# Rebuilding the first layer's attention: both branches of a head at once, stacked float32r scores, mask on TensorE, division by fours of heads, adaLN rows shared between engines

## The chip, the core and the metric

The kernel runs on one core of a Trainium2 chip. A core has five engines, each with an instruction queue of its own that is worked off in order: TensorE (PE, matrix products; PEld is its weight load), VectorE (DVE), ScalarE (ACT), GpSimd (POOL) and SyncE (SP, which here issues the DMA transfers). The metric is the device time of one execution in microseconds (us).

## What is computed

A stack of four layers on 256 tokens of 1024 features, all float32. The change is in the first: adaLN, a "native sparse" attention with three branches, and an output projection.

```python
h = rms_norm(x, g) * (1 + scale) + shift      # shift, scale, gate = silu(c) @ w_ada + b_ada
u = h @ w_in                                  # q, k/v of three branches, z, gate logits
q: 16 heads of 64;  k, v: 2 groups of 8 heads
o_cmp = softmax(q k_cmp^T, 15 compressed keys) v_cmp
o_slc = softmax(rope(q) rope(k_s)^T, causal) v_s     # all blocks are selected at this length
o_win = softmax(rope(q) rope(k_w)^T, causal) v_w     # the window is longer than the text
o = gates[0] * o_cmp + gates[1] * o_slc + gates[2] * o_win
x = x + gate * ((o * silu(z)) @ w_out)
```

With 256 tokens the second and third branch have the same form and the same causal mask and differ in keys and values alone. While the heads run, the kernel also makes the rows of adaLN that come next: 1024 columns each of the first layer's gate and the second layer's scale and shift, silu(c) @ w + b.

## The kernel before

**Weights.** Products with weights are made of float32r parts: `make` loads a unit of 1024 floats per partition (512 KB, tile `wr`), ACT copies it to the high part (`wh`, L210), DVE subtracts for the low part (`wl`, L211), and three products add up (L239, L240, L243). Five units are loaded ahead and eight split ahead. All loads are issued by SP in order; a load whose buffer is still read holds those behind it.

**Order.** The code is emitted in program order, and a scheduler puts each instruction into its engine's queue by priority; `first(ATTN)` moves the heads' instructions 1200 places ahead of what was emitted before, so that dense products (of z) fill in between. Within a queue nothing overtakes.

**The stage before the heads.** q is copied from PSUM, rotated (`rope`: three products on DVE and a sum, L408, on POOL where it is 512 wide), and both q (`qp`) and rotated q (`qr`) are transposed, four 128-blocks at a time. Keys are rotated and transposed into `kT`. Compressed keys (`kbd`) and values (`vbd`) come from small products. `cmp_probs(tok, g)` gives the probabilities of a group's eight heads over compressed keys, transposed (`cT`); it runs for group 1 before the heads and for group 0 in the middle of group 1.

**A head** (`nsa_head`). For each of two branches: `scores` does one fp32 product for the first block of 128 queries (128 keys) and one for the second (256 keys), with 64 contraction rows (L417). `shifted` (L427) adds the mask, negates and takes the least value in one DVE instruction per block, with a read of the accumulator. `exps` (L433) runs on ACT with a sum as a by-product. The sums are inverted, multiplied by the gates, and each probability block is scaled, 128 columns on DVE (L830), 256 on ACT (L828). `av` transposes three blocks (L440), copies them from PSUM on ACT (L443) and does three products with the values (L446 to L448) into `o`, where all branches and eight heads of a group add up, the compressed branch first (`cmp_part`, L808).

**AdaLN rows** (`ada_rows`, `ada`). A half row (512 columns) is a sum over eight chunks of 128 features. A transfer holds two chunks (512 KB, tile `ar`, L542), and `ARAW = 3` of them are loaded ahead through three buffers. A call of `ada` does one item: two scaled additions on DVE (L562, L564) into `ac`, and the load that takes the freed buffer. After four items one product with ones (L569) sums over partitions, and DVE adds the bias. There are 24 items; two follow each head of group 1, one each head of group 0.

**After the heads.** o is multiplied by silu(z) in `zs` (L856), transposed (L289), split, and `project_out` multiplies it by `w_out` (first product L239). Then the second layer begins, with dense products.

Of the kernel before, what the change touches and what calls it, by code (L numbers as in the profile page):

```python
# [8 lines left out]
F32 = mybir.dt.float32  # L9
# [7 lines left out]
D = 1024  # L17
# [77 lines left out]
def body(ctx: ExitStack, tc: tile.TileContext, A: dict, out: bass.AP, stop=None):  # L95
# [17 lines left out]
    # ---- PSUM banks: each kind of tile goes round its own banks  # L113
# [12 lines left out]
    # ---- constants  # L126
# [15 lines left out]
    junk = cp.tile([128, D], BF, name="junk")  # L142
# [36 lines left out]
    # ---- weights: streamed in order, split exactly into two float32r parts  # L179
    specs, made = [], []  # L180
    state = {"next": 0, "live": 0, "gate": None, "hold": False, "group": 2}
# [17 lines left out]
    def make():  # L199
# [11 lines left out]
        dve.tensor_sub(lo, raw[:, :nk * n], hi.bitcast(F32))  # L211
# [35 lines left out]
    def dense_cols(xts, nk, n, sink, kind="mm"):  # L247
        """a group of n columns of x @ W, block of tokens after block of tokens; the sink takes them from PSUM"""
# [10 lines left out]
    # ---- transposed operands  # L259
# [25 lines left out]
    def to_T(src, n, xt, k0):  # L285
        """n blocks of 128 columns, transposed and split, to chunks k0.. of xt"""
# [9 lines left out]
    def transposes(dst, srcs, eng, width=128):  # L296
        """up to four [128, width] blocks, transposed to dst [width, n, 128]"""
# [12 lines left out]
    # ---- norms  # L310
# [6 lines left out]
    def rms_rstd(src, n, eps=1e-6):  # L317
        s = small(1)
        act.activation(junk[:, :n], src, AF.Square, accum_out=s)
        return rstd_of(s, 1.0 / n, eps)  # L320
# [4 lines left out]
    def deepnorm(layer, which, last=False):  # L325
        """the sink of a product that closes a sublayer: x <- LN(alpha x + p) * g + b, and its transposed parts"""
# [28 lines left out]
    def gated(tok, h, p, g, tp):  # L355
        """x += p * g"""
# [4 lines left out]
    def halves_sumsq(tok, h, s):  # L361
        act.activation(junk[:, half(h)], x[tok][:, half(h)], AF.Square, accum_out=s[:, h:h + 1])
# [28 lines left out]
    # ---- rotations  # L391
# [3 lines left out]
    def rope(dst, src, H, hd, cos, sin, tp):  # L395
        """dst = rotated src; src [128, H, 2*hd], dst the same or with copies side by side"""
# [26 lines left out]
    def shifted(s, added, n2, tp, scale=1.0):  # L423
        """-scale * (s + added), and its least value of each block of queries"""
# [11 lines left out]
    def av(e, v, o, c0, start, eng, tp, stop=True):  # L436
        """o[tok][:, c0:c0+64] += e of the block times v(block of keys)"""
# [93 lines left out]
    def ada_rows(rows, new, ahead):  # L531
# [13 lines left out]
        def step(after=None):  # L545
# [20 lines left out]
            if u < 3:  # L566
                return
# [291 lines left out]
    for _ in range(24):  # L859
        ada()  # L860
# [438 lines left out]
```

## Time and profile before

| | |
|---|---|
| median of three runs | 1026.41 us (1024.37, 1026.41, 1039.41) |
| profiled execution, span | 1024.7 us |
| PE busy | 978.7 us, 96% |
| DVE busy | 662.3 us, 65% |
| ACT busy | 508.4 us, 50% |
| POOL busy | 39.0 us, 4% |

The profile shows one execution by its span; what a run's time has beyond it is 1.7 us against the median. Busy shares are means over stages that have different limits, so the stretches are read one by one: up to 60 us the first adaLN rows and columns, 60 to 105 rotations and compression, 105 to 210 the heads, and from there the projection and the other layers. A row of the timeline gives start, length, engine, line, operation, what it writes and reads, how many instructions are joined, and in brackets the idle time ahead of it with what ended it.

### The profile page before, as it was taken

The page shows a single profiled execution, that of the slowest core. Times are in us where ns is not written, and L with a number is a line of the kernel's source. Part 1 is how long each engine was busy: PE and PEld are TensorE (multiplying, and loading weights), DVE is VectorE, ACT ScalarE, POOL GpSimd, SP SyncE. Part 2 cuts the span into 40 slices and gives each one's busy share as a digit, 9 for nine tenths or more (in the row PEclk, how much of TensorE's full clock was granted, in tenths as well). Part 3 has the DMA queues.
Part 4 walks back from the last instruction along what each step waited for, and adds up shares of the span by engine and source line. Part 5 has one row for each costly group of instructions (what it writes and reads, how often), then busy time and mean ns, then how long its engine had stood idle before and what let it go on. Part 6 is the DMA issues. An engine that isn't in the chain of part 4 may idle for free.

```text
span 1024.7 us, 16049 instructions
## 1 busy us (share of the span) xinstructions
PE 978.7 (96%) x6068; PEld 852.1 (83%) x6068; DVE 662.3 (65%) x1304; ACT 508.4 (50%) x967; POOL 39.0 (4%) x41
## 2 busy tenths in 40 slices
PE   5988999999999999999999999999999999999997
PEld 5877687777777878978899999978997789999995
DVE  5888788848776678665855555476454495544554
ACT  5584566734545536584343443335664344433440
POOL 1002000001220001000000000000000000000000
PEclk9998898999999999999999999999999999999999
DMA  9995776434865335632356455556543335455441
GB/s 287 309 308 182 249 241 201 129 101 134 261 191 179 119 102 190 229 103 64 99 208 205 165 194 206 176 171 190 170 145 99 112 117 192 165 202 189 165 144 42
DMA packets 106173, 177.75 MB, mean 173 GB/s; under 512 B 8816, under 2 KB 40688, under 8 KB 106096
## 3 DMA queue, kind: packets, MB, share of 16 engines
q1 hardware_dynamic: 106096, 176.72, 53.5%
q8 instruction: 48, 0.79, 0.3%
q14 instruction: 29, 0.24, 0.1%
HBM read 175.65 MB, written 1.05 MB: 172 GB/s over the span
## 4 chain that ended last, share of the span: by engine, by line
PE 83%; DVE 8%; DMA 4%; ACT 3%; issue 1%; SPq 0%; DVEq 0%; POOL 0%; ACTq 0%; POOLq 0%
PE ps L239 13%; PE ps L240 13%; PE ps L243 13%; PE ps L277 9%; PE ps L278 9%; PE ps L279 9%; PE ps L417 6%; PE ps L440 2%; DMA wr<-in_ada_w_dram 2%; PE ps L446 2%; DVE wl L211 2%; PE ps L447 2%; PE ps L448 2%; PE ps L289 1%; PE ps L300 1%
## 5 line engine op out<-in xcount | busy, mean ns | idle before, releaser
L211 DVE TENSOR_TENSOR wl<-wr,wh 128x1024 fp32r<-128x1024 f32 (+5 forms) x276 | 322.9, 1204 | 155.1 <-ACT wh L210 153.9
L210 ACT ACTIVATE wh<-wr 128x1024 fp32r<-128x1024 f32 (+5 forms) x276 | 270.5, 1022 | 168.2 <-PE ps L243 74.8
L277 PE MATMUL ps<-xh,wh 128*128 128x256 f32 x736 | 209.1, 284 | 0.0
L279 PE MATMUL ps<-xh,wl 128*128 128x256 f32 x736 | 208.9, 284 | 0.0
L278 PE MATMUL ps<-xl,wh 128*128 128x256 f32 x736 | 208.5, 283 | 0.0
L240 PE MATMUL ps<-wl,xh 128*128 128x512 f32 (+5 forms) x544 | 201.3, 373 | 0.4 <-DVE wl L211 0.4
L239 PE MATMUL ps<-wh,xh 128*128 128x512 f32 (+5 forms) x544 | 197.8, 376 | 3.9 <-ACT xh L292 2.6
L243 PE MATMUL ps<-wh,xl 128*128 128x512 f32 (+5 forms) x544 | 173.4, 372 | 1.0 <-DVE xl L293 0.8
L277 PEld LDWEIGHTS ps<-xh,wh 128*128 128x128 f32 x736 | 141.1, 192 | 0.5
L278 PEld LDWEIGHTS ps<-xl,wh 128*128 128x128 f32 x736 | 141.1, 192 | 0.3
L279 PEld LDWEIGHTS ps<-xh,wl 128*128 128x128 f32 x736 | 141.1, 192 | 0.1
L239 PEld LDWEIGHTS ps<-wh,xh 128*128 128x128 f32 x544 | 104.3, 193 | 22.7 <-ACT xh L292 6.2
L240 PEld LDWEIGHTS ps<-wl,xh 128*128 128x128 f32 x544 | 105.7, 194 | 16.1 <-issue 1.2
L243 PEld LDWEIGHTS ps<-wh,xl 128*128 128x128 f32 x544 | 101.1, 192 | 18.4 <-DVE xl L293 2.9
L239 PE MATMUL ps<-wh,hh 128*128 128x512 f32 x176 | 68.6, 390 | 0.0
L240 PE MATMUL ps<-wl,hh 128*128 128x512 f32 x176 | 68.6, 390 | 0.0
L243 PE MATMUL ps<-wh,hl 128*128 128x512 f32 x176 | 68.5, 389 | 0.0
L433 ACT ACTIVATE e<-e,sm 128x128 f32<-128x128 f32 x112 | 49.7, 446 | 19.7 <-DVE sm L427 19.5
L427 DVE CUSTOM_DVE_ANT_0 e<-ps,mask 128x128 f32<-128x128 f32 (+1 forms) x144 | 45.2, 352 | 20.4 <-PE ps L417 11.4
L292 ACT ACTIVATE xh<-ps 128x512 fp32r<-128x512 f32 x36 | 20.9, 597 | 75.0 <-PE ps L289 74.7
L314 POOL TENSOR_TENSOR sm<-sm,nhalf 128x1 f32<-128x1 f32 x18 | 12.7, 706 | 856.0 <-DVE sm L313 856.0
L564 DVE SCALAR_TENSOR_TENSOR ac<-ar,cs,ac 128x512 f32<-128x512 f32 x56 | 41.7, 745 | 1.0 <-DMA ar<-in_ada_w_dram 0.7
(319 smaller groups left out, 1230.8 us busy)
## 6 DMA issues: line engine op xcount, KB each, us to landing
wr<-in_ffn_w_gate_dram SPq DMA_DIRECT2D x44, 512.0 KB, 4.7
wr<-in_ffn_w_up_dram SPq DMA_DIRECT2D x44, 512.0 KB, 4.7
wr<-in_ffn_w_down_dram SPq DMA_DIRECT2D x44, 512.0 KB, 4.7
ar<-in_ada_w_dram SPq DMA_DIRECT2D x32, 512.0 KB, 4.5
wr<-in_dil_w_in_dram SPq DMA_DIRECT2D x32, 512.0 KB, 4.5
wr<-in_cd_w_in_dram SPq DMA_DIRECT2D x22, 512.0 KB, 4.7
wr<-in_ada_w_dram SPq DMA_DIRECT2D x32, 256.0 KB, 5.1
wr<-in_nsa_w_in_dram SPq DMA_DIRECT2D x12, 512.0 KB, 5.5
```

The source lines that it names most:

```text
L210: act.activation(hi, raw[:, :nk * n], AF.Copy)
L211: dve.tensor_sub(lo, raw[:, :nk * n], hi.bitcast(F32))
L239: pe.matmul(p, lhsT=xt[0][:, k, :], rhs=w[0][:, kw, c], start=start and t == 0, stop=False)
L240: pe.matmul(p, lhsT=xt[0][:, k, :], rhs=w[1][:, kw, c], start=False, stop=False)
L243: pe.matmul(p, lhsT=xt[1][:, k, :], rhs=w[0][:, kw, c], start=False, stop=stop and t == n - 1)
L277: pe.matmul(o, lhsT=w[0], rhs=xh[:, k, :], start=k == 0, stop=False)
L278: pe.matmul(o, lhsT=w[0], rhs=xl[:, k, :], start=False, stop=False)
L279: pe.matmul(o, lhsT=w[1], rhs=xh[:, k, :], start=False, stop=k == 7)
L417: pe.matmul(p[:, c0:c1], lhsT=qT(tok), rhs=kT[:, :c1 - c0], start=True, stop=masks is None)
L427: state["dve"] = dve.tensor_tensor_reduce(out=e[:, c0:c1], in0=s[:, c0:c1], in1=added[:, 256 - (c1 - c0):], scale=-scale, scalar=3e38, op0 ...
L433: act.activation(e[:, c0:c1], e[:, c0:c1], AF.Exp, bias=n2[:, i:i + 1], scale=-1.0, accum_out=den[:, i:i + 1])
L564: dve.scalar_tensor_tensor(ac, raw[:, j, :], cs[:, k:k + 1], ac, op0=ALU.mult, op1=ALU.add)
```

## The change

**Scores.** Rotated q is split into a high and a low float32r part that lie side by side per head, so that a transpose gives 128 rows, [high; low], of one head (`qhl`). Keys of both branches stand twice along the rows, in a high (`kh`) and a low part (`kl`). A head's scores of a block of queries for both branches are one product with `kh`, one with `kl` and one bf16 product that adds the mask (`identb` times `causal01`). Two heads go together (`nsa_pair`), over three PSUM banks: `x` for the second block of each head, `y` for the first blocks of both.

**Softmax.** Three DVE reductions per pair give the maxima, and the exponentials read PSUM directly. Probabilities are not scaled: each head and branch has columns of its own in `o` for four heads, and `nsa_close` divides: a reciprocal, gates, one product per block of tokens, additions to the compressed part `oc` (on POOL for group 1, on DVE for group 0), and the product with `zs`. Of four copies of transposed probabilities three are on DVE.

**Compressed branch.** All four `cmp_probs` come before the heads.

**AdaLN rows.** 48 items of 256 KB, one chunk each, through three buffers as before; the first three chunks of a half row are scaled on ACT in place and added on POOL, the other five stay on DVE. Six items follow each pair, in program order, and no longer behind a named DVE instruction. **w_out**: the low parts of its eight units are made on POOL (`slow` is that matrix). `rms_rstd` works in two halves.

```diff
-        dve.tensor_sub(lo, raw[:, :nk * n], hi.bitcast(F32))
+        (pool if W is slow else dve).tensor_sub(lo, raw[:, :nk * n], hi.bitcast(F32))
...
-        items = [(r, h, u) for r in rows for h in range(2) for u in range(4)]
+        items = [(r, h, u) for r in rows for h in range(2) for u in range(8 // wide_k)]
...
+                    if k < shared:
+                        act.activation(raw[:, j, :], raw[:, j, :], AF.Copy, scale=cs[:, k:k + 1])
+                        if k == 1:
+                            pool.tensor_add(ac, at["r0"], raw[:, j, :])
+                        elif k:
+                            pool.tensor_add(ac, ac, raw[:, j, :])
+                        at["r0"] = raw[:, j, :]
+                    elif k == 0:
...
-        transposes(qr[tok][g], blocks(qq), dve)
+        flat = wide("hl")
+        hl = flat.rearrange("p (h a d) -> p h a d", h=8, a=2)
+        act.activation(hl[:, :, 0].bitcast(F32R), by_head(qq), AF.Copy)
+        dve.tensor_sub(hl[:, :, 1], by_head(qq), hl[:, :, 0])
+        for i in range(2):
+            transposes(qhl[tok][g][:, i * 4:i * 4 + 4, :], [flat[:, (i * 4 + j) * 128:(i * 4 + j + 1) * 128] for j in range(4)], (act, dve)[i])
...
+    with first(ATTN):
+        for g in (1, 0):
+            for tok in range(2):
+                cmp_probs(tok, g)
...
+    def nsa_scores(g, hh):
+        xs, y = [ps("x"), ps("x")], ps("y")
+        for j in range(2):
+            for tok, (p, n) in enumerate(((y[:, j * 256:(j + 1) * 256], 128), (xs[j], 256))):
+                q = qhl[tok][g][:, hh + j, :]
+                p3 = p.rearrange("p (b k) -> p b k", b=2)
+                pe.matmul(p3, lhsT=q, rhs=kh[:, g, :, :n], start=True, stop=False)
+                pe.matmul(p3, lhsT=q, rhs=kl[:, g, :, :n], start=False, stop=False)
+                pe.matmul(p3[:, :, n - 128:n], lhsT=identb, rhs=causal01.to_broadcast([128, 2, 128]), start=False, stop=True)
+        return xs, y
...
-                   lambda: pC.tile([128, D], F32, tag="araw", bufs=ARAW, name=nm("ar")), ARAW)
+                   lambda: pC.tile([128, 512], F32, tag="araw", bufs=ARAW, name=nm("ar")), ARAW, 1, 3)
...
-            for hh in range(8):
-                nsa_head(g, hh, o)
-                for _ in range(1 + g):
-                    ada(state["dve"])
+            for quad in range(2):
+                o = [ps("o"), ps("o")]
+                den = pC.tile([128, 2, 4, 2], F32, tag="den", bufs=2, name=nm("den"))
+                for pair in range(2):
+                    nsa_pair(g, quad * 4 + pair * 2, den, o)
+                    for _ in range(6):
+                        ada()
+                nsa_close(g, quad, den, o, pool if g else dve)
```

How the queues change is shown at three places. DVE's queue before, in the early heads of group 1: the scaled additions (L564, two per `ar` tile) stand between masked reductions (L427) of several heads, with weight splits (L211) among them.

```order
L211 TENSOR_TENSOR wl_1280<-wr_1277,wh_1279 128x1024
L427 ISA e_1371,sm_1370<-ps_1367,mask 128x128
L427 ISA sm_1370 128x1
L427 ISA e_1371,sm_1370<-ps_1367,mask 128x256
L427 ISA sm_1370 128x1
L564 SCALAR_TENSOR_TENSOR ac_1347<-ar_1166,cs,ac_1347 128x512 x2
L473 SCALAR_TENSOR_TENSOR zs_120<-th_1295,ps_1246 128x512
L564 SCALAR_TENSOR_TENSOR ac_1347<-ar_1350,cs,ac_1347 128x512
L211 TENSOR_TENSOR wl_1292<-wr_1289,wh_1291 128x1024
L819 RECIPROCAL sm_1357<-sm_1356 128x4
L427 ISA e_1417,sm_1416<-ps_1413,mask 128x128
L427 ISA sm_1416 128x1
```

DVE's queue in the changed kernel, after the copies of the first pair's transposed probabilities (`eT`, L451): the first half row's five scaled additions (L577, one per `ar` tile), the first steps of a division, then the next pair's copy and the reductions (L864, L862) of the pair after it.

```order
L451 COPY eT_1451<-ps_1447 128x384
L451 COPY eT_1460<-ps_1456 128x384
L577 SCALAR_TENSOR_TENSOR ac_1468<-ar_1470,cs,ac_1468 128x512
L880 RECIPROCAL rd_1578<-den_1399 128x16
L577 SCALAR_TENSOR_TENSOR ac_1468<-ar_1474,cs,ac_1468 128x512
L884 TENSOR_TENSOR rd_1578<-rd_1578,gates 128x8 x2
L577 SCALAR_TENSOR_TENSOR ac_1468<-ar_1478,cs,ac_1468 128x512
L577 SCALAR_TENSOR_TENSOR ac_1468<-ar_1481,cs,ac_1468 128x512
L577 SCALAR_TENSOR_TENSOR ac_1468<-ar_1484,cs,ac_1468 128x512
L451 COPY eT_1526<-ps_1522 128x384
L864 TENSOR_REDUCE sm_1610<-ps_1595 128x2
L862 TENSOR_REDUCE sm_1610<-ps_1597 128x4
```

The five additions of a half row now each name another `ar` tile and stand in one run ahead of a copy and of the reductions of the pair that follows.

SP's queue before, where the loads of adaLN rows begin.

```order
L205 DMA wr_1829<-in_nsa_w_out_dram 128x2x512
L542 DMA ar_1162<-in_ada_w_dram 128x2x512
L542 DMA ar_1164<-in_ada_w_dram 128x2x512
L542 DMA ar_1166<-in_ada_w_dram 128x2x512
L542 DMA ar_1350<-in_ada_w_dram 128x2x512
L205 DMA wr_1841<-in_nsa_w_out_dram 128x2x512
L542 DMA ar_1354<-in_ada_w_dram 128x2x512
L205 DMA wr_1853<-in_nsa_w_out_dram 128x2x512
L205 DMA wr_1865<-in_nsa_w_out_dram 128x2x512
L542 DMA ar_1402<-in_ada_w_dram 128x2x512
L205 DMA wr_2323<-in_dil_w_in_dram 128x2x512
```

SP's queue in the changed kernel at the same place.

```order
L207 DMA wr_1825<-in_nsa_w_out_dram 128x2x512
L548 DMA ar_1305<-in_ada_w_dram 128x512
L548 DMA ar_1307<-in_ada_w_dram 128x512
L548 DMA ar_1309<-in_ada_w_dram 128x512
L548 DMA ar_1470<-in_ada_w_dram 128x512
L548 DMA ar_1474<-in_ada_w_dram 128x512
L548 DMA ar_1478<-in_ada_w_dram 128x512
L548 DMA ar_1481<-in_ada_w_dram 128x512
L548 DMA ar_1484<-in_ada_w_dram 128x512
L548 DMA ar_1487<-in_ada_w_dram 128x512
L548 DMA ar_1555<-in_ada_w_dram 128x512
L207 DMA wr_1837<-in_nsa_w_out_dram 128x2x512
```

A load was two chunks and has become one; twice as many stand between the loads of `w_out` and of the next layer (`wr`).

POOL's queue before, from the last rotation of the first layer on: nothing stands between that and the second layer's small powers (L314) and rotations (L408).

```order
L408 TENSOR_TENSOR q_881<-rt_883,rt_884 128x512
L408 TENSOR_TENSOR q_950<-rt_952,rt_953 128x512
L314 TENSOR_TENSOR sm_2411<-sm_2411,nhalf 128x1
L314 TENSOR_TENSOR sm_2468<-sm_2468,nhalf 128x1
L408 TENSOR_TENSOR qq_2558<-rt_2559,rt_2560 128x512
```

POOL's queue in the changed kernel after the same rotation (now L414).

```order
L414 TENSOR_TENSOR q_988<-rt_990,rt_991 128x512
L570 TENSOR_TENSOR ac_1468<-ar_1305,ar_1307 128x512
L572 TENSOR_TENSOR ac_1468<-ac_1468,ar_1309 128x512
L213 TENSOR_TENSOR wl_1349<-wr_1346,wh_1348 128x1024
L213 TENSOR_TENSOR wl_1361<-wr_1358,wh_1360 128x1024
L213 TENSOR_TENSOR wl_1373<-wr_1370,wh_1372 128x1024
L570 TENSOR_TENSOR ac_1563<-ar_1487,ar_1555 128x512
L213 TENSOR_TENSOR wl_1385<-wr_1382,wh_1384 128x1024
L572 TENSOR_TENSOR ac_1563<-ac_1563,ar_1558 128x512
L891 TENSOR_TENSOR oc_1303<-oc_1303,nt_1582 128x256 x2
```

The additions of adaLN rows (L570, L572), the low parts of `w_out` (L213) and the closing additions (L891) stand one behind the other there, three low parts ahead of the second half row's first addition.

## Rows read from the trace of the kernel before

**Rows 1.** The page's chain of work that ended last: shares by engine.

```profile
PE 83%; DVE 8%; DMA 4%; ACT 3%; issue 1%; SPq 0%; DVEq 0%; POOL 0%; ACTq 0%; POOLq 0%
PE ps L239 13%; PE ps L240 13%; PE ps L243 13%; PE ps L277 9%; PE ps L278 9%; PE ps L279 9%; PE ps L417 6%; PE ps L440 2%; DMA wr<-in_ada_w_dram 2%; PE ps L446 2%; DVE wl L211 2%; PE ps L447 2%; PE ps L448 2%; PE ps L289 1%; PE ps L300 1%
```

**Rows 2.** Busy us by stretch (length, PE, PEld, DVE, ACT, POOL, granted clock, DMA).

```profile
60.00:105.00 45.00, 37.41 (x224) 30.91 (x222) 39.19 (x61) 29.09 (x49) 7.51 (x4) 0.92 0.72 226
105.00:210.00 105.00, 100.43 (x566) 76.51 (x567) 84.80 (x293) 69.51 (x219) 0.00 (x0) 0.90 0.60 195
210.00:320.00 110.00, 108.39 (x516) 85.95 (x515) 81.52 (x128) 54.60 (x90) 16.23 (x10) 1.00 0.57 177
```

**Rows 3.** The same columns for two stretches within the heads.

```profile
111.00:119.00 8.00, 8.00 (x28) 6.19 (x27) 5.49 (x23) 3.39 (x11) 0.00 (x0) 0.50 0.52 182
160.00:169.00 9.00, 9.00 (x32) 6.57 (x32) 5.56 (x23) 5.17 (x19) 0.00 (x0) 0.51 0.71 226
```

**Rows 4.** Timeline of PE, from the rotations to the output projection.

```profile
79.88 1.12 PE L300 MATMUL ps<-ident,q 128*128 128x128 f32 x4 [6.06 <-POOL q L408]
...
105.37 0.41 PE L784 MATMUL ps<-kbd,qp 128*128 128x30 f32 x2 [1.26 <-ACT kbd L764]
...
108.84 2.76 PE L417 MATMUL ps<-kT,qr 64*128 64x128 f32 x8 [0.36 <-DVE vbd L773]
...
146.94 1.57 PE L417 MATMUL ps<-kT,qr 64*128 64x128 f32 x8
...
173.47 0.93 PE L417 MATMUL ps<-kT,qr 64*128 64x128 f32 x8
...
176.97 0.92 PE L417 MATMUL ps<-kT,qr 64*128 64x128 f32 x4
...
210.50 1.04 PE L289 MATMUL ps<-ident,zs 128*128 128x128 f32 x8
211.79 0.50 PE L239 MATMUL ps<-wh,xh 128*128 128x512 f32 x1 [0.25 <-ACT xh L292]
...
212.36 0.39 PE L239 MATMUL ps<-wh,xh 128*128 128x512 f32 x1
212.59 0.39 PE L240 MATMUL ps<-wl,xh 128*128 128x512 f32 x1
```

**Rows 5.** Groups by line and shape on DVE, 105 to 225 us: busy, mean ns | idle.

```profile
L564 DVE SCALAR_TENSOR_TENSOR ac<-ar,cs,ac 128x512 f32<-128x512 f32 x42 | 31.3, 746 | 0.2
L211 DVE TENSOR_TENSOR wl<-wr,wh 128x1024 fp32r<-128x1024 f32 x12 | 14.7, 1221 | 3.5 <-ACT wh L210 3.3
L427 DVE CUSTOM_DVE_ANT_0 e<-ps,mask 128x256 f32<-128x256 f32 x32 | 13.4, 419 | 0.0
...
L856 DVE TENSOR_TENSOR zs<-ps,zs 128x512 f32<-128x512 f32 x4 | 2.6, 681 | 0.0
```

**Rows 6.** The same on ACT.

```profile
L443 ACT ACTIVATE eT<-ps 128x384 f32<-128x384 f32 x32 | 14.5, 485 | 14.4 <-PE ps L440 14.2
L828 ACT ACTIVATE e<-e,sm 128x256 f32<-128x256 f32 x32 | 14.4, 498 | 2.6 <-DVE sm L821 2.4
```

**Rows 7.** Timeline of POOL: rotation additions of 512 columns.

```profile
82.93 1.30 POOL L408 TENSOR_TENSOR q<-rt,rt 128x512 f32<-128x512 f32 x1 [3.11 <-DVE rt L403]
85.72 2.70 POOL L408 TENSOR_TENSOR q<-rt,rt 128x512 f32<-128x512 f32 x1 [1.49 <-DVE rt L403]
```

**Rows 8.** Timeline of DVE beside the second of these.

```profile
87.16 2.34 DVE L211 TENSOR_TENSOR wl<-wr,wh 128x1024 fp32r<-128x1024 f32 x1
```

**Rows 9.** Transfers: times issued, KB each, median us from issue to landing.

```profile
ar<-in_ada_w_dram SPq DMA_DIRECT2D x32, 512.0 KB, 4.5
...
wr<-in_nsa_w_in_dram SPq DMA_DIRECT2D x8, 256.0 KB, 4.2
...
bias<-in_rel_ext_dram SPq DMA_DIRECT2D x8, 128.0 KB, 3.0
```

**Rows 10.** Tile ar: idle time of its reader (us, times) that a transfer ended.

```profile
  DMA ar<-in_ada_w_dram: 0.7, 1
```

More of the change, by code (lines that the diff above doesn't have):

```diff
@@ L317, in rms_rstd @@
     def rms_rstd(src, n, eps=1e-6):
-        s = small(1)
-        act.activation(junk[:, :n], src, AF.Square, accum_out=s)
-        return rstd_of(s, 1.0 / n, eps)
+        s = small(2)
+        for i in range(0, n, 512):
+            m = min(512, n - i)
+            act.activation(junk[:, :m], src[:, i:i + m], AF.Square, accum_out=s[:, i // 512:i // 512 + 1])
+        if n > 512:
+            dve.tensor_add(s[:, 0:1], s[:, 0:1], s[:, 1:2])
+        return rstd_of(s[:, 0:1], 1.0 / n, eps)
     def half(h):
@@ L529, in body, with ada_rows @@
     arow = {}
-    def ada_rows(rows, new, ahead):
-        items = [(r, h, u) for r in rows for h in range(2) for u in range(4)]
+    def ada_rows(rows, new, ahead, wide_k=2, shared=0):
+        items = [(r, h, u) for r in rows for h in range(2) for u in range(8 // wide_k)]
         raws, at = [], {"i": 0}
@@ L565, in step @@
             load()
-            if u < 3:
+            if u < 8 // wide_k - 1:
                 return
@@ L704, in body @@
     cmQ, pQ = opened("nsaQ")
+    qp = [[pQ.tile([128, 4, 128], F32, name=f"qp{t}{g}") for g in range(2)] for t in range(2)]
     def k_side(p, tok, a, b, i):
@@ L709, in k_side @@
         rope(r, p[:, a:b].rearrange("p (g d) -> p g d", g=2), 2, 32, tab(C_COSK, tok, 64), tab(C_SINK, tok, 64), pQ)
-        transposes(kT[:, 2 * i:2 * i + 2, tok * 128:(tok + 1) * 128],
-                   [r[:, g].rearrange("p a d -> p (a d)") for g in range(2)], act)
+        pt = ps("pt")
+        for g in range(2):
+            pe.transpose(pt[:, g * 128:(g + 1) * 128], r[:, g].rearrange("p a d -> p (a d)"), ident)
+        v = pt[:, :256].rearrange("p (g t) -> p g t", g=2)
+        hi, lo = (t[:, :, i, tok * 128:(tok + 1) * 128] for t in (kh, kl))
+        act.activation(hi, v, AF.Copy)
+        dve.tensor_sub(lo, v, hi.bitcast(F32))
     def q_side(tok, g, p):
@@ new lines, in cmp_probs, with cmp_part @@
+        act.activation(cT[tok][g][:120], pT[:120, :128], AF.Copy)
+    with first(ATTN):
+        for g in (1, 0):
+            for tok in range(2):
+                cmp_probs(tok, g)
+    closed(cmQ)
+    closed(cmB)
+    cmC, pC = opened("nsaC")
+    zs = [pC.tile([128, D], F32, name=f"zs{t}") for t in range(2)]
+    ocmp = [pC.tile([128, 512], F32, name=f"oc{t}") for t in range(2)]
+    def cmp_part(g, tok):
+        p = ps("pt")
+        pe.matmul(p, lhsT=cT[tok][g][:120], rhs=vbd[g][:120].rearrange("p h d -> p (h d)"), start=True, stop=True)
+        act.activation(ocmp[tok], p, AF.Copy)
@@ new lines, in body @@
+    causal01 = mask[:, None, 128:256]
+    def nsa_scores(g, hh):
[8 more added lines that the diff above has]
+        return xs, y
@@ L833, in body @@
     oxt = [None, None]
     ada = ada_rows((("gate0", 0, 2 * D), ("scale", 1, D), ("shift", 1, 0)),
-                   lambda: pC.tile([128, D], F32, tag="araw", bufs=ARAW, name=nm("ar")), ARAW)
-    assign(mm=[0], s=[1, 2, 3], pt=[4, 5], o=[6, 7])
-    with first(ATTN):
-        probs = [cmp_probs(tok, 1) for tok in range(2)]
+                   lambda: pC.tile([128, 512], F32, tag="araw", bufs=ARAW, name=nm("ar")), ARAW, 1, 3)
+    assign(mm=[0], x=[1, 2], y=[3], pt=[4, 5], o=[6, 7])
     for g in (1, 0):
-        o = [ps("o"), ps("o")]
@@ L843, in body @@
             for tok in range(2):
[L844 to L850 removed]
+                cmp_part(g, tok)
+            for quad in range(2):
[6 more added lines that the diff above has]
+                nsa_close(g, quad, den, o, pool if g else dve)
             if g == 0:
@@ L853, in body @@
                 for tok in range(2):
-                    to_T(zs[tok][:, half(1)], 4, oxt[tok], 4)
-            for tok in range(2):
-                dve.tensor_mul(zs[tok][:, half(g)], o[tok], zs[tok][:, half(g)])
-                if g == 0:
-                    to_T(zs[tok][:, half(0)], 4, oxt[tok], 0)
-    for _ in range(24):
+                    for i in range(2):
+                        to_T(zs[tok][:, half(1 - i)], 4, oxt[tok], 4 - 4 * i)
+    for _ in range(48):
         ada()
```

99 lines of the change are left out of this document (50 added, 49 removed).

## Prediction

> **What bounds the kernel now.** First the chain of waits: TensorE (PE) holds 83% of it and the wait for an adaLN transfer in the opening stage 2% [rows 1]. So a microsecond that PE loses or gains counts nearly one for one, unless PE is waiting in that stretch. Next the busy time by stretch [rows 2], which tells where it waits. From 60 to 105 us (rotations and compression) PE is busy 37.4 of 45 us and VectorE (DVE) 39.2: DVE and what hangs on it set the pace. From 105 to 210, the heads, PE is busy 100.4 of 105, DVE 84.8, ScalarE (ACT) 69.5, GpSimd (POOL) 0. After 210 PE is busy 108.4 of 110. The change ends where that begins, so its worth is the shift of one event: the first product of the output projection, now at 211.79 us [rows 4]. What follows is dense PE work that has no slack to give or take.
>
> In the heads PE ran 17 us at half clock, 0.50 from 111 to 119 and 0.51 from 160 to 169 [rows 3], the 1.2 GHz level of the two; at the other level that work takes some 8.5 us less. PE's own need in 105 to 210 is then about 92 us, not 100. Last the rows of PE [rows 4]: the first scores stand at 108.84, and a head without other work between comes 3.50 us after the one before (173.47 to 176.97).
>
> **The change part by part.** *PE.* Scores of both branches of a head cost 1.57 us now (146.94) where both branches of one head run one after the other, 0.92 for one branch alone (176.97), but also 0.93 for eight such records in a row (173.47) [rows 4]. New: per head one 512-column and one 256-column block of float32r for each part of the keys, and bf16 mask products. A 512-column float32r product comes 0.23 us after the one before (212.36, 212.59 in [rows 4]), so 2 x 0.23 + 2 x 0.12 + the masks, estimated as at most the same again for two quarter passes, 0.23: about 0.93. Gain per head 0 to 0.65 us, 0 to 10 us in 16 heads; I take 0.6, 9.6 us, as the 1.57 rows are the plain case. Sixteen more transposes before the heads (four in 1.12 us at 79.88 [rows 4], so 4.5 us at most) lie in the 7.6 us that PE is not busy in that stage.
>
> *The stage before the heads.* Four splits of rotated queries (512 wide, as L856, 0.68 us [rows 5]) are 2.7 us of DVE; four subtractions for the low part of keys, half as wide (0.4 estimated), 1.6. DVE is the busiest there, and one PE wait of 6.06 us ends on POOL's rotation add behind DVE (79.88 [rows 4]), so I charge all 4.3. All four blocks of compressed probabilities now precede the heads, not two. The two took 105.37 to 108.84, 3.5 us [rows 4]; two more, half overlapped, 1.7. First scores at 108.84 + 6.0 = about 115. Bounds: +1 (the 5.8 us that DVE is not busy in that stage take nearly all) and +10 (nothing overlaps).
>
> *Per head on DVE and ACT.* DVE loses the masked reduction (0.42 us and a narrower one each branch [rows 5]) and the small reciprocals; it gains three reductions of 512 columns a pair of heads (0.68 by L856, 2.0 together) and three of four transposed copies, about 0.55 each. ACT loses 32 scalings of 0.50 (L828 [rows 6]) and three quarters of the copies of 0.49 (L443), and gains 18 scalings of 512 columns, about 0.7 each from the 0.50 for 256. Over the stage the three engines each need about 70 to 80 us. That is less than 105, and none of it decides, if the next part is right.
>
> *AdaLN's rows.* This is where I see the path. Before: 24 transfers of 512 KB in the heads through three buffers, each consumed by two DVE instructions of 0.75 [rows 5]. They landed in 4.5 us [rows 9], and DVE waited for one but once, 0.7 us [rows 10]: three buffers held enough work. After: 48 transfers of 256 KB, still three buffers, so half as much work in flight, and a half row is a chain of eight items: chunks 0 to 2 scaled on ACT and added on POOL, chunks 3 to 7 on DVE. A buffer's next load cannot start before its reader is done. Following one buffer after another, a half row holds three landings in series, one POOL add, two DVE steps and one ACT scaling. Landing time L of 256 KB: the nearest rows are 4.2 us (256 KB of the same queue), 3.0 (128 KB), 4.5 (512 KB) [rows 9]; I take 3.5, between the first two, as the stretch is less crowded than the opening, and keep 3.0 to 4.2. POOL's add of 512 columns: 1.3 alone, 2.7 beside a DVE subtraction [rows 7]; I take 1.3. So 3 x 3.5 + 1.3 + 2 x 0.75 + 0.7 = 14.0 us per half row of eight, and 10.5 per pair of heads, which has six. DVE's queue is in order, and in the listing of it the steps of a pair stand between the copies of one pair and the reductions of the next: while DVE waits for a landing, the next pair's reductions, exponentials and AV wait; while it does those reductions, no item is freed. So 10.5 + 2.0 = 12.5 us per pair, against 7.0 for two plain heads now and 13.1 with everything that ran between (105 us over 8 pairs).
>
> The Trainium skill, "DMA: Bandwidth & Descriptors", section on the anatomy of one DMA, gives about 2.0 us fixed plus bytes over 436 GB/s, fitted on another issue path, and its bandwidth section advises 1 MiB or more per transfer; that speaks against halving these loads. By its figure 256 KB would be 2.6 us as an estimate, a pair 10.5 and the whole about 1016; the 4.2 us row differs, and the row decides.
>
> *Splits of the output weights to POOL* take eight DVE subtractions of 1.22 [rows 5] out of the heads. On POOL, twice a 512 add, each is 2.6 alone. Three stand ahead of the second half row's first add in POOL's queue, so they delay the ring there once, some 4 us, which is hidden as far as PE's first z products fill in. I charge 0 and keep it in the range.
>
> *The close.* Division, two products of 0.68 and four additions for the last four heads: about 3 us on DVE, of which I charge 1, since the first of two blocks goes on while the other is transposed; then the eight transposes and the split, 1.3 from 210.50 to 211.79 [rows 4], with the last product before them 1.5.
>
> **Sum.** 115 + 8 x 12.5 + 1 + 1.5 = 217.5, against 211.8: +5.7 us. The profiled span is 1024.7, the median of the runs 1026.41, 1.7 above it, which I take as what lies around the span. 1024.7 + 5.7 + 1.7 = **1032 us**. All PE savings are in it as waiting.
>
> **Rivals.** (A) The ring is hidden: landings of 3.0 or less, or loads far enough ahead that DVE never waits, as now [rows 10]. Then PE sets the stage: 92 us at full clock, less 9.6 of scores, 82, from 110 or 115: project_out at 192 to 197 plus 2.5, so -17 to -12, 1009 to 1014; with all ends at their best (first scores at 110, no term for the close, and two compressed blocks, about 1 us each, out of the heads) 1005. Against it: three buffers of half the size. (B) POOL decides: 12 adds at 2.7 instead of 1.3 add 1.4 to both adds of a half row, and eight splits of twice that width take 5.4 instead of 2.6 and stand among the adds in its in-order queue; DVE, whose next steps wait for those adds, holds the heads. DVE pays too: the L211 at 87.16 lasts 2.34 us beside POOL's add [rows 8], where the mean is 1.22 [rows 5]. Price per pair 0.75 x 1.4 x 2 = 2.1, and a share of (8 x 2.8)/8 = 2.8 for the splits, half on the path, 1.4: +3.5 per pair, +28 in all; with half of that 1046, with all 1060. It passes 2% where pairs take 1.9 us more than forecast, 14.4. Against it: the reductions and copies of DVE read PSUM, and a scaled addition of 0.75 is short, so an add meets few of them.
>
> The Trainium skill, "SBUF — State Buffer", section on who interferes with whom, says that a DVE instruction with two SBUF inputs and a GpSimd one that reads SBUF exclude each other for a whole instruction. The trace agrees for these rows: 1.30 against 2.70 [rows 7]. DVE's scaled additions read two SBUF tensors, so by that rule (B) rather than the 1.3 would hold wherever they meet an add.
>
> (C) The stacked scores gain nothing, because two branches already ran in 0.93 [rows 4]: on my path that changes nothing, on (A) it adds 10, 1019 to 1024.
>
> More idle PE may also draw more half-clock stretches. PE needs some 80 of the 102 us forecast; each stretch of 9 us at 0.5 uses up 4.5 of that slack, so four of them are free.
>
> **Chances.** Forecast, 1020 to 1044: 0.52. (A) 0.20, of it 0.11 below 1006. (C), with the ring hidden: 0.08. (B) 0.20, of it 0.17 above 1047. Two per cent of the median, about what a measurement can tell, is 20.5 us: faster than 1005.9 0.11, slower than 1046.9 0.17, between 0.72. The range that leaves out 2 in 10, from the bounds L = 3.0 (12.5 a half row, 9.4 + 2 a pair: 208.7, 1023; first scores at +1 as well: 1018; and rival A) and L = 4.2 (16.1, 14.1 a pair: 230, 1045; with part of B): **1007 to 1051**. The likeliest's own: 1020 to 1044.
>
> **What would show it.** Right: DVE's scaled additions wait for transfers of adaLN rows, tens of microseconds in the heads, a pair of heads lasts about 12 us, first scores at about 115, PE busy under 85% there, and the output projection starts at 215 to 220. Landings near 3.5 would confirm the chain, POOL adds near 1.3 rule out (B). Wrong: no such waits, pairs of 7 to 9 us and a projection before 200 mean (A); POOL adds of 2 and more with DVE waiting on POOL rather than transfers mean (B). If the first scores stand later than 120, the stage before was under-priced, whatever the heads do.

## The result and the profile after

| | before | after |
|---|---|---|
| median of four runs | 1025.39 us (1021.58 to 1039.41) | 1049.63 us (1048.15 to 1056.25) |
| profiled span | 1024.7 us | 1047.5 us |
| ratio after to before | | 1.0258 (1.0219 to 1.0297) |

The ratio is of fast runs alone: of the four runs of the kernel before, the one of 1039.41 us was a slow one. The change makes the kernel 24 us slower. The forecast had been 1032 us, with a chance of 0.72 that the change stays within 2%. The page's first section of the changed kernel has less PE work in a longer span:

```profile
PE 975.2 (93%) x6052; PEld 851.8 (81%) x6052; DVE 670.1 (64%) x1176; ACT 500.1 (48%) x945; POOL 82.6 (8%) x69
```

Busy time by stretch of the changed kernel, columns as in [rows 2]: up to the first scores, the heads, and behind them.

```profile
105.00:121.20 16.20, 13.53 (x84) 11.68 (x85) 7.88 (x25) 5.06 (x19) 0.00 (x0) 0.73 0.26 87
121.20:234.20 113.00, 87.20 (x481) 68.16 (x479) 81.04 (x130) 55.14 (x174) 43.25 (x28) 0.86 0.52 168
234.20:320.00 85.80, 84.22 (x389) 66.05 (x390) 66.10 (x104) 38.97 (x62) 12.90 (x8) 1.00 0.56 184
```

The third row is as dense as its fellow in [rows 2]: all of the loss lies ahead of the output projection. Timeline of PE in the changed kernel (as [rows 4]):

```profile
111.97 0.41 PE L806 MATMUL ps<-kbd,qp 128*128 128x30 f32 x2 [0.36 <-DVE vbd L799]
...
121.22 1.20 PE L853 MATMUL ps<-kh,qhl 128*128 128x256 f32 x1
...
146.52 0.90 PE L446 MATMUL ps<-ident,e 128*128 128x128 f32 x3 [4.36 <-DVE eT L451]
...
181.34 0.69 PE L452 MATMUL ps<-vW,eT 128*128 128x64 f32 x2 [7.37 <-DVE eT L451]
...
234.25 0.50 PE L241 MATMUL ps<-wh,xh 128*128 128x512 f32 x1 [0.47 <-ACT xh L294]
```

The projection starts at 234.25 instead of 211.79, +22.5 us: first scores at 121.22 instead of 108.84 (+12.4), and heads of 113.0 us instead of 103.0 (+10.1). (One block of scores had run ahead of all this, at 102.25; first scores are here those behind which the others follow.) Twice PE waits long for a copy of transposed probabilities, which stands in VectorE's queue. The chain of waits over the heads, by line, says behind what; beside it the same view of the kernel before, from its first scores on.

```profile
by line: DMA ar<-in_ada_w_dram 35.1%; DVE ac L577 16.0%; issue 9.5%; ACT ar L568 4.8%; ACT e L871 3.6%; ACT e L869 2.7%; PE ps L841 2.6%; POOL ac L572 2.3%; DVE oc L891 2.0%; PE ps L452 1.8%; PE ps L582 1.6%; DVE eT L451 1.5%; PE ps L454 1.
```

```profile
by line: PE ps L417 24.6%; PE ps L440 10.0%; PE ps L446 9.1%; PE ps L239 7.6%; PE ps L448 7.1%; PE ps L447 7.1%; PE ps L569 6.3%; PE ps L240 6.1%; PE ps L243 6.1%; PE ps L808 3.7%; PE ps L784 3.7%; ACT eT L443 3.5%; ACT e L433 1.3%; issue 1
```

Before, the chain is PE's own work. After, it is adaLN's rows: their transfers, VectorE's scaled additions (L577), ScalarE's scalings (L568) and GpSimd's additions. Tile `ar` of the changed kernel (idle us of its readers, times):

```profile
L548 SPq DMA_DIRECT2D ar<-in_ada_w_dram x56: 327/328/1428, 124.9 to 342.8; - x56
L577 DVE SCALAR_TENSOR_TENSOR ac<-ar,cs,ac x44: 651/752/2845, 135.5 to 351.6; 128x512 f32<-128x512 f32 x44
...
  DMA ar<-in_ada_w_dram: 33.2, 18
...
DMA to landing us min/median/max: 2.5/3.1/7.6
```

33.2 us in 18 waits stand where [rows 10] had 0.7 in one; 15.5 of them are VectorE's additions, 17.7 ScalarE's scalings. The Trainium skill, "DMA: Bandwidth & Descriptors", section on the anatomy of one DMA, would give 2.6 us for 256 KB as an estimate, by a fit made on another issue path; 3.1 was measured, with a shortest of 2.5. And VectorE's additions are not 0.75 us as in [rows 5]. Groups by shape on VectorE, then its timeline, then GpSimd's, all of the changed kernel:

```profile
L577 DVE SCALAR_TENSOR_TENSOR ac<-ar,cs,ac 128x512 f32<-128x512 f32 x30 | 33.4, 1113 | 15.0 <-DMA ar<-in_ada_w_dram 14.8
```

```profile
141.58 4.42 DVE L577 SCALAR_TENSOR_TENSOR ac<-ar,cs,ac 128x512 f32<-128x512 f32 x3
145.91 0.55 DVE L451 COPY eT<-ps 128x384 f32<-128x384 f32 x1
...
173.82 7.00 DVE L577 SCALAR_TENSOR_TENSOR ac<-ar,cs,ac 128x512 f32<-128x512 f32 x3 [6.55 <-DMA ar<-in_ada_w_dram]
180.74 0.55 DVE L451 COPY eT<-ps 128x384 f32<-128x384 f32 x1
```

```profile
131.63 1.27 POOL L570 TENSOR_TENSOR ac<-ar,ar 128x512 f32<-128x512 f32 x1 [38.61 <-ACT ar L568]
...
136.36 7.51 POOL L213 TENSOR_TENSOR wl<-wr,wh 128x1024 fp32r<-128x1024 f32 x3 [2.09 <-ACT wh L212]
...
152.19 2.39 POOL L213 TENSOR_TENSOR wl<-wr,wh 128x1024 fp32r<-128x1024 f32 x1 [1.77 <-ACT wh L212]
...
172.40 10.63 POOL L213 TENSOR_TENSOR wl<-wr,wh 128x1024 fp32r<-128x1024 f32 x4
```

GpSimd is hardly slowed: an addition takes 1.27 us, a low part 2.39 beside PSUM work of VectorE and 2.5 to 2.7 on average in the runs of three and four. VectorE is slowed: three additions take 7.00 us beside GpSimd's 10.63, and the 30 of them 33.4 us, 11 more than at 0.746. Both long waits of PE end on the copy that stands right behind such additions (145.91 and 180.74). The Trainium skill, "SBUF — State Buffer", section on who interferes with whom, says that a VectorE instruction with two SBUF inputs and a GpSimd one that reads SBUF exclude each other for whole instructions; the trace agrees, and shows who pays where long GpSimd instructions meet short ones of VectorE.

**An account of the stage.** From 105 us to the first product of the projection, the length is a sum of three parts: PE's idle time (length less PE busy), the clock loss (half of the time in which PE was busy at the 1.2 GHz level), and the rest, PE's work at full clock. The stretches at that level are read from the trace. Those of the changed kernel, with 32.6 us of PE busy in 41.0:

```profile
112.40:122.60 10.20, 10.05 (x53) 8.51 (x52) 5.70 (x27) 1.59 (x6) 0.00 (x0) 0.50 0.00 0
146.50:153.30 6.80, 5.84 (x23) 4.82 (x24) 3.79 (x7) 5.29 (x14) 2.39 (x2) 0.50 0.94 292
177.20:187.50 10.30, 6.16 (x27) 5.45 (x28) 10.09 (x13) 1.97 (x6) 5.83 (x3) 0.50 0.61 190
197.70:211.40 13.70, 10.60 (x47) 8.86 (x45) 7.56 (x14) 6.89 (x22) 4.01 (x4) 0.50 0.50 155
```

| kernel (profiled run, its time) | length | idle | clock loss | work | median |
|---|---|---|---|---|---|
| before (span 1024.7) | 106.8 | 4.8 | 10.2 | 91.7 | 1025.4 |
| after (1049.3) | 129.3 | 28.5 | 16.3 | 84.4 | 1049.6 |
| e1 low parts on VectorE (1043.0) | 125.0 | 23.3 | 16.3 | 85.4 | 1042.5 |
| e9 attention alone (1037.4) | 116.4 | 16.6 | 15.8 | 84.0 | 1035.0 |
| e17 attention, small ring (1054.2) | 134.9 | 22.4 | 27.4 | 85.1 | 1047.6 |
| e7 before, new rows (1045.6) | 125.5 | 11.1 | 21.5 | 92.9 | 1045.1 |
| e14 before, new rows, six buffers (1040.5) | 123.0 | 8.0 | 23.9 | 91.1 | 1043.5 |
| e13 before, 256 KB, VectorE (1021.3) | 104.0 | 5.4 | 5.1 | 93.4 | 1021.2 |

The profiled run of e17 is the slowest of its four, so its row is not the typical one. The change saves 7.3 us of PE work. Idle time takes 23.7 back, and the clock 6.1 more.

### The profile page after: what moved, and what is told of

The parts are those of the page before. It is cut to its first block, busy times and chain, and to the rows that moved or that the text cites. A ratio compares the mean times of both kernels' runs of the same rounds, so it can differ in the third digit from the quotient of the medians.

```text
span 1047.5 us, 15969 instructions
## 1 busy us (share of the span) xinstructions
PE 975.2 (93%) x6052; PEld 851.8 (81%) x6052; DVE 670.1 (64%) x1176; ACT 500.1 (48%) x945; POOL 82.6 (8%) x69
## 4 chain that ended last, share of the span: by engine, by line
PE 72%; DVE 11%; DMA 8%; ACT 4%; issue 3%; POOL 1%; SPq 0%; DVEq 0%; ACTq 0%; POOLq 0%
PE ps L241 12%; PE ps L242 11%; PE ps L245 11%; PE ps L279 8%; PE ps L280 8%; PE ps L281 8%; DMA ar<-in_ada_w_dram 4%; PE ps L423 3%; DMA wr<-in_ada_w_dram 2%; DVE wl L213 2%; DVE ac L577 2%; PE ps L446 2%; ACT wh L212 1%; PE ps L302 1%; PE ps L291 1%
## 5 line engine op out<-in xcount | busy, mean ns | idle before, releaser
L213 DVE TENSOR_TENSOR wl<-wr,wh 128x1024 fp32r<-128x1024 f32 (+5 forms) x268 | 312.5, 1202 | 151.0 <-ACT wh L212 150.4
L241 PEld LDWEIGHTS ps<-wh,xh 128*128 128x128 f32 x544 | 103.5, 191 | 23.3 <-ACT xh L294 7.4
L446 PE MATMUL ps<-ident,e 128*128 128x128 f32 x240 | 44.2, 294 | 11.4 <-ACT oc L842 4.5
L577 DVE SCALAR_TENSOR_TENSOR ac<-ar,cs,ac 128x512 f32<-128x512 f32 x44 | 43.8, 995 | 15.9 <-DMA ar<-in_ada_w_dram 15.5
L446 PEld LDWEIGHTS ps<-ident,e 128*128 128x128 f32 x240 | 31.7, 165 | 16.6 <-ACT oc L842 5.8
```

Source lines behind the costliest of these rows:

```text
L213: (pool if W is slow else dve).tensor_sub(lo, raw[:, :nk * n], hi.bitcast(F32))
L241: pe.matmul(p, lhsT=xt[0][:, k, :], rhs=w[0][:, kw, c], start=start and t == 0, stop=False)
L446: pe.transpose(p[:, i * 128:(i + 1) * 128], e[:, i * 128:(i + 1) * 128], ident)
L577: dve.scalar_tensor_tensor(ac, raw[:, j, :], cs[:, k:k + 1], ac, op0=ALU.mult, op1=ALU.add)
```

## The experiments

Ratios are to runs of the kernel before on the same chip, with a 95% interval. First the parts undone in the changed kernel.

**e1**: low parts back on VectorE. **e2**: five buffers for rows. **e3**: both.

```diff
-        (pool if W is slow else dve).tensor_sub(lo, ...)
+        dve.tensor_sub(lo, ...)                                      e1, e3
-   pC.tile([128, 512], tag="araw", bufs=ARAW), ARAW, 1, 3)
+   pC.tile([128, 512], tag="araw", bufs=5), 5, 1, 3)                 e2, e3
-   eT bufs=3; nt a tile of its own
+   eT bufs=2 in the heads; nt shares the buffer of th                e2, e3: room
```

> The changed kernel with the low parts of the output weights back on VectorE. Theory L (lock): in the changed kernel VectorE's scaled additions and gate products stretch while GpSimd makes low parts (three additions in 7.00 us instead of 2.0, three in 4.42, a pair of tiny products in 2.42); these stretches sum to about 12 us and TensorE idles 7.4 and 4.4 us behind them. L expects 9 to 13 us less than the changed kernel, 1037 to 1041, no stretched addition, and no idle time of TensorE over 5 us in the heads. Theory R (ring): three buffers of half the size set the pace whatever GpSimd does; R expects 1046 to 1050.

> The changed kernel with five buffers of 256 KB for adaLN rows instead of three (the closing products' buffer is shared with that of the tanh, and two transposed-probability buffers instead of three make room). Theory R: the adaLN row's first readers idle 33 us for transfers over the stage; five buffers halve that and the time falls by 8 to 15 us, to 1035 to 1042. Theory L: the waits for transfers are mostly beside other work; 0 to 4 us, 1046 to 1050. A third theory, S (late start): the ring's first transfer is issued at 124.9 us, 16.4 later than before, as its memory is that of the compressed branch's temporaries; S expects at most 5 us from deeper buffers.

> Both edits at once: low parts on VectorE and five buffers. L and R together, if they add up: 1024 to 1032. If they are the same time counted twice: as the better of the two alone, about 1037. S expects 10 us or more of loss against the kernel before to remain, 1035 and up.

Measured: e1 1042.5 (1.0179, 1.0154 to 1.0205), 7.2 less. VectorE's additions in e1:

```profile
L577 DVE SCALAR_TENSOR_TENSOR ac<-ar,cs,ac x44: 657/746/1206, 138.0 to 347.9; 128x512 f32<-128x512 f32 x44
```

The longest takes 1.21 us instead of 2.85, and the four above 0.76 all stand beside GpSimd's closing additions (L891). The edit left transfers and buffers as they were, and yet transfers hold 9.6% of the chain over the heads instead of 35.1%. e2 1047.7 (1.0236), e3 1046.1 (1.0218, 1.0177 to 1.026), though waits for rows fell from 33.2 to 15.3 and, in e3, 6.7 us. The low parts on GpSimd are worth 7 us. Deeper buffers take most of the waits away and hardly any time; but the room for them came from one of the three buffers of transposed probabilities (and e4 and e12 below do the same), and what that costs alone was not run.

**e4**: only group 1's compressed probabilities ahead of the heads. **e12**: that and e1.

```diff
-        for g in (1, 0): ... cmp_probs(tok, g)
+        cmp_probs(tok, 1)           # group 0's after the first four heads of group 1
```

> The changed kernel with only group 1's compressed probabilities ahead of the heads, group 0's behind the first four heads, as before the change (same room-making as with five buffers, but three buffers). S: first scores come at 112 to 115 instead of 121.2 and the first adaLN row transfer at 109 to 113 instead of 124.9; the time falls by 7 to 12 us, 1038 to 1043. L and R: the heads' end is set by the ring or the lock; R expects the earlier start of the ring to be worth nearly all of 12 us too; L expects less than 5, 1045 to 1050.

> The changed kernel with low parts on VectorE and only group 1's compressed probabilities ahead of the heads (three buffers of 256 KB). The first alone gave 1042.5, the second 1048.8 with a profile at 1044.6. If both act on different waits: 1034 to 1039. If they act on the same: 1041 to 1044. Half-clock time in the stage, 41 us in the changed kernel and 21 before, should follow the idle time of TensorE.

Measured: e4 1048.8 (1.0237), e12 1041.7 (1.0164), within 1 us of the same kernels without the edit, with first scores at 116.58 in e4 and 118.45 in e12, 4.6 and 4.9 us earlier than without it. An earlier start was worth nothing there.

**e5**: no rows among the heads, all behind them. **e10**: that with low parts on VectorE. **e11**: the same of the kernel before.

```diff
-                    for _ in range(6):
-                        ada()
```

> The changed kernel with no step of adaLN's rows among the heads: all 48 come behind them, so the time as a whole must rise; read are the heads alone, from the first scores to the first product of the output projection, 113 us in the changed kernel and 103 before. Theory B (the attention's own chain, with two heads at a time on three banks that are held until the exponentials have read them): a pair stays at 10 us or more, heads of 85 us and up. Theory I (the in-order queues: steps of adaLN's rows that wait stand ahead of the attention's copies, reductions and exponentials): without them a pair takes 7 to 9 us, heads of 60 to 75 us.

> The rebuilt attention with low parts on VectorE and no step of adaLN's rows among the heads, all behind them; the heads alone are read. Theory B: 80 to 92 us from the first scores to the first product of the output projection, 10 us and more a pair. Theory I: 60 to 75 us.

> The kernel before with no step of adaLN's rows among the heads, all behind them; the heads alone are read, 103 us with them. Full-speed work of TensorE there is about 85 us, so 88 to 98 us if TensorE sets its pace. If this is no longer than the rebuilt attention without rows, the rebuilt one has lost its saving to its own chain.

Read are the heads. e5: 122.93 to 212.22, 89 us. e10:

```profile
122.50:209.00 86.50, 74.88 (x470) 61.06 (x468) 57.53 (x109) 49.42 (x165) 11.40 (x12) 0.91 0.37 119
```

86.5 us, 10.8 a pair, PE idle 11.6: the rebuilt attention is not the 60 to 75 us that theory I expected. The rows among the heads add 23.7 us in the changed kernel (113.0 against 89.3 in e5). e11 gives no yardstick: its two times are 1050.75 and 1070.65, and its profile had 0.78 of the clock in the stage.

**e6**: rows in the old form, 512 KB, VectorE. **e9**: that and e1, so the attention alone.

```diff
-   pC.tile([128, 512], tag="araw", bufs=ARAW), ARAW, 1, 3)
+   pC.tile([128, D], tag="araw", bufs=ARAW), ARAW, 2, 0)             3 steps a pair, not 6
-   aacc bufs=2; eT bufs=3; nt
+   aacc bufs=1; eT bufs=2; nt shares th                              room
```

> The changed kernel with adaLN's rows in their old form: 24 transfers of 512 KB, both chunks on VectorE, three buffers of twice the size, three steps a pair (room made by one buffer less for transposed probabilities and sums, and a shared one at the close). Theory R/I: steps that seldom wait and none on ScalarE or GpSimd; 10 to 18 us less than the changed kernel, 1032 to 1040. Theory B: within 4 us, 1046 to 1050.

> The rebuilt attention alone: adaLN's rows in their old form (512 KB, VectorE, three buffers) and the low parts of the output weights on VectorE. If the attention by itself is worth its 11 us of TensorE work less the later first scores (+12): 1022 to 1028. If its own chain costs more than it saves (theory B): 1034 to 1040. If the parts' losses simply added up (20 for the rows and 4.6 for the splits, measured alone on the kernel before), nothing would be left for it: 1024.

Measured: e6 1043.9 (1.0203), e9 1035.0 (1.0104, 1.0061 to 1.0147). Read as steps: attention alone +12, low parts on GpSimd +9 more (e9 to e6), new rows +6 more (e6 to after). The last step is not clear of noise: the ratios of e6 (1.0159 to 1.0247) and of the changed kernel (1.0219 to 1.0297) overlap.

Now the parts alone on the kernel before.

**e7**: new rows. **e8**: low parts on GpSimd. **e13**: 256 KB, three buffers, all on VectorE. **e14**: shared, six buffers. **e15**: six buffers, all on VectorE.

```diff
+   pC.tile([128, 512], tag="araw", bufs=3), 3, 1, 3)     e7; e13: 3, 1, 0; e14: 6, 1, 3; e15: 6, 1, 0
-                for _ in range(1 + g):
+                for _ in range(2 + 2 * g):                e7, e13 to e15
```

> The kernel before with adaLN's rows alone in the new form: 48 transfers of 256 KB through three buffers, the first three chunks of a half row on ScalarE and GpSimd; four steps a head in group 1, two in group 0. Theory R: the ring of half the size holds the old attention too; 8 to 16 us slower than before, 1032 to 1040. Theory B: the old attention, whose scores leave their bank at once, has slack for it; within 4 us, 1020 to 1028.

> The kernel before with the low parts of the output weights alone on GpSimd. Theory L: scaled additions stretch beside them, VectorE loses some 10 us in the heads, of which TensorE feels part: 4 to 9 us slower, 1028 to 1033. If the lock hurts only together with the rest of the change: within 2 us, 1022 to 1026.

> The kernel before with 48 transfers of 256 KB through three buffers, all chunks on VectorE (new form of adaLN's rows, 1045 us, with the sharing undone). If the ring's size costs: 1038 to 1046. If the sharing costs: 1023 to 1029.

> The kernel before with adaLN's rows in the new, shared form but six buffers of 256 KB, as many bytes as the old ring (1045 us with three). If the ring's size costs: 1024 to 1030. If the sharing costs: 1038 to 1046.

> The kernel before with 48 transfers of 256 KB through six buffers, all on VectorE: only the transfer size is new. If twice as many, smaller transfers cost by themselves: 1028 and up. If not: 1021 to 1026, as before.

Measured: e7 1045.1 (1.0219, 1.0147 to 1.0291); e8 1029.3 (1.0049, 1.0028 to 1.007); e13 1021.2 (0.9975, 0.9957 to 0.9993); e14 1043.5 (1.0183); e15 1027.1 (1.0029). There the size of the ring costs nothing. Undoing the sharing of the first chunks with ScalarE and GpSimd gives back 24 us with three buffers (e7 to e13) and 16 with six (e14 to e15). Against the kernel before, PE's work in e7 and e14 is the same and its idle time only 3 to 6 us longer; 11 to 14 us are clock. This is not one trace's accident: the mean clock was 0.956 to 0.972 in all eight runs of e7 and e14, and 0.983 to 0.989 in the ten of e13. In e14, ScalarE's timeline, PE's, and busy time by stretch:

```profile
160.63 0.72 ACT L562 ACTIVATE ar<-ar,cs 128x512 f32<-128x512 f32 x1 [1.20 <-issue]
161.26 0.42 ACT L811 ACTIVATE cT<-ps 120x128 f32<-120x128 f32 x2
```

```profile
161.57 0.88 PE L440 MATMUL ps<-ident,e 128*128 128x128 f32 x6 [1.69 <-ACT cT L811]
```

```profile
163.00:198.00 35.00, 35.00 (x112) 23.69 (x111) 21.10 (x74) 19.65 (x63) 4.41 (x4) 0.51 0.45 145
```

A scaling of rows that starts late (what held it, the trace does not show) holds a copy behind it in ScalarE's queue, and PE stands for 1.69 us. Some 2 us later its clock falls to the 1.2 GHz level, for 34 us in which PE is busy throughout. That the wait brings the fall is not shown by this order alone. e13 has no such stretch; its only one at half clock is 108.9 to 119.1, at the start of its heads:

```profile
105.00:208.95 103.95, 98.57 (x581) 74.86 (x579) 87.57 (x298) 71.47 (x225) 0.00 (x0) 0.95 0.60 198
```

Last, whether sharing is also the cost inside the changed kernel, and the late start. **e16**: all chunks on VectorE, three buffers of 256 KB. **e17**: that and e1. **e18**: e17 with the compression and its weights ahead of group 0's queries.

```diff
-   bufs=ARAW), ARAW, 1, 3)
+   bufs=ARAW), ARAW, 1, 0)                                           e16 to e18
-    dense_cols(xt, 8, 512, lambda tok, p: q_side(tok, 0, p))         ahead of compress(0), compress(1)
+    dense_cols(xt, 8, 512, lambda tok, p: q_side(tok, 0, p))         behind them: e18
```

> The changed kernel with all eight chunks of a half row on VectorE, three buffers of 256 KB as in the change: sharing alone undone, 1049.6 with it. If sharing costs here as on the kernel before: 1030 to 1036. If it costs only what old rows gave back (1043.9 with 512 KB): 1041 to 1046. If the small ring is what costs here: 1047 and up.

> The same, and the low parts of the output weights on VectorE: what is left is the attention and the small ring. The attention with 512 KB rows gave 1035.0. If the small ring costs nothing: 1032 to 1037. If it costs: 1040 and up.

> The same as the second, and the order of the stage before the heads turned: the compression and its weights ahead of group 0's queries, so that its small transposes no longer stand behind the transposes of split queries. If the late start is that queue: first scores 4 to 7 us earlier and 1028 to 1032. If it is the work itself on VectorE and ScalarE: first scores as late as without it (122 to 124 us) and the time within 3 us of the second kernel.

Measured: e16 1050.6 (1.0259), e17 1047.6 (1.0224, 1.0182 to 1.0265), e18 1047.7 (1.0238). None is as the theory of sharing expected. In the changed kernel, undoing it gave nothing back: +1.0 us (after to e16) and +5.2 (e1 to e17, intervals overlapping). e17 is 12.6 us slower than e9, which has transfers and buffers of 512 KB, takes half as many steps, and gave up other buffers for room. Tile `ar` of e17, idle us of its readers:

```profile
  DMA ar<-in_ada_w_dram: 11.5, 13
```

against one wait of 3.5 in e9. e18 starts the heads at 120.30, 4.2 us before e17 (124.55), and takes as long by its median (1047.7 and 1047.6), so here too an earlier start was worth nothing. Where the heads end can't be compared, as e17's profile is of its slowest run.

## Why the prediction failed

**The ring in the heads: right in kind.** The forecast saw VectorE waiting for rows of half the size, in order ahead of the next pair's copies. The waits (33.2 us) and the chain (35.1% transfers) show it, and e17 against e9 (12.6 us) fits it. That half the bytes in flight are the cause is not shown: five buffers took most of the waits and hardly any time (e2, e3), and e1 took most of the transfers off the chain without touching them. Landings of 3.1 us lie in its bounds and below its 3.5. The pair came to (234.25 - 121.22) / 8 = 14.1 us with the close in it; the forecast's 102.5 us for the same stretch make 12.8.

**The step that failed in the heads is "I charge 0" for the low parts on GpSimd.** Rival (B) had the right pair of engines, but put its price on GpSimd: GpSimd's additions stayed at 1.3 (one at 1.6), and VectorE's, which it names only in passing ("DVE pays too"), stretched by 11 us. Undone in e1, the heads are 6.3 us shorter, 0.8 a pair of the missing 1.3, and the whole is 7 us faster; alone on the kernel before the low parts cost 5 us (e8), with old rows 9 (e9 to e6).

**First scores: term mis-sized, 6.0 for 12.4.** Compressed scores start 6.6 later (111.97 for 105.37), where 4.3 had been charged for work on VectorE. The four blocks then take 9.25 us where two took 3.5, so 5.8 more instead of 1.7: no overlap is left, and from 112.4 on PE ran them at 0.50. That is the prediction's own sign, "later than 120, the stage before was under-priced". In other kernels with this stage (e1, e2, e3, e5, e6, e9, e10) first scores stand between 122.2 and 126.2, so the 12.4 of one trace is at the low end; e18 moves them by 4.2 us by the order of the work alone. A start that is late also delays the ring, whose buffers come free only behind the last of those blocks: first load at 124.9 instead of 108.5 by the tile's rows, which the forecast put at the first scores without saying so. What the start costs alone can't be read from e4, e12 or e18, where moving it gave nothing; in e9, where rows seldom wait, it is the larger part: first scores 14.4 late, heads 4.8 shorter.

**The clock: "four of them are free" is not borne out.** PE's busy time at half clock in the stage rose from 20.5 to 32.6 us, which by the account is 6.1 us of the 22.5. No run took the half clock away by itself, so what other waiting would have hidden of it is open. But time and clock go together among runs of one kernel: the changed one took 1048.15 us at a mean clock of 0.973 and 1056.25 at 0.967. Two of its stretches:

```profile
147.00:153.00 6.00, 5.06 (x21) 4.14 (x21) 2.99 (x7) 4.99 (x14) 2.09 (x2) 0.50 0.93 291
...
181.00:188.00 7.00, 6.66 (x31) 5.95 (x32) 6.33 (x11) 2.47 (x9) 2.03 (x1) 0.54 0.66 201
```

They go with the waits of 4.36 and 7.37 us above, and a third with one of 2.67; waits of 1.80 and 1.45 us were followed by none. PE is fully wanted just then, so the slack that the forecast counted on lies elsewhere. A long wait is not the only thing that brings such a stretch: in the kernel before, one came where the longest wait of the 20 us ahead of it was 0.58 us.

```profile
160.20:170.50 10.30, 10.30 (x39) 7.83 (x41) 6.86 (x25) 4.97 (x18) 0.00 (x0) 0.50 0.63 202
```

**PE savings: right in kind**, 9.6 us forecast, 7.3 by the account (6.3 to 7.7 in e1, e9 and e17), and no gain in time, as the forecast said. **Rivals**: (A) and (C), which need a ring that is hidden, fell, as DVE waits. **Size**: 217.5 forecast for the projection, 234.25 measured; 16.8 apart, 6.2 from the first scores, and 10.6 from the heads. That 1049.6 still lies inside the stated 1007 to 1051 is in part luck: the upper end was made of landings of 4.2 us, which were 3.1.

**What stays open.** Of the 17.6 us between the forecast and the median, e1 shows 7; the rest is not taken apart by any run. Why sharing costs 16 to 24 us on the kernel before and nothing inside the changed one is only argued: before, steps stand singly among heads, and the small ring never holds them long; after, six stand in a run, and ScalarE takes some of it off VectorE's queue. By the same account, idle and clock loss of e3 stayed at 21.9 and 16.7 us with five buffers, and what else holds its heads was not taken apart; the chain there still has 16.0% transfers. The attention's own 10.8 us a pair was not either; that three PSUM banks are held until the exponentials have read them fits it and was not tried.

A version a little ahead of both is e13, 0.9975 (0.9957 to 0.9993): halved transfers, all on VectorE, in the old attention, with 5.1 us of clock loss in place of 10.2.

## What to carry to other kernels

Work taken from a busy engine pays only where what then ends last is shorter; price each moved instruction by who stands behind it in the new queue, and long two-input GpSimd work by what it does to VectorE, not to itself. A ring of small buffers cost nothing where its steps were spread singly among other work (e13); where they stand in a run the kernel with it was 12.6 us slower (e9 to e17), but more buffers did not mend the changed kernel, so count who stands behind each step and not the bytes alone. Do not count on slack of PE to hide time at half clock: in e7 and e14, 3 to 6 us more idle time came with 11 to 14 us more clock loss.

## What the runs showed of the hardware

A wait of PE of 1.69 us was followed by 35 us at 0.51 of the clock with PE busy for all 35.00 (e14); with waits of 4.36 and 7.37 us in the changed kernel the stretches were 6.8 and 10.3 us, and in the kernel before one of 10.3 us came without a long wait. Runs of one and the same kernel differ with it: the kernel before took 1020.57 us at a mean clock of 0.988 and 1028.43 at 0.976. A 256 KB transfer landed in 2.5 us at the least and 3.1 in the middle, where 512 KB took 4.5 before. GpSimd's 1024-column subtraction took 2.39 us beside PSUM work of VectorE and at most 2.85 with one of VectorE's two-input instructions let in, which itself took up to 2.85 us instead of 0.75.
